# Two layers with three mixers on one core: the shared key and gate-rank product with both weight parts side by side, the latents' squares added on GpSimd, and another order of steps

## The chip, the cores and the metric

The kernel runs on one core of a Trainium2 chip. Its time is the device time of one execution in microseconds. The trace is one execution taken by the hardware profiler; its span is the time from the first to the last instruction that it records.

## What is computed

Two layers (256 tokens, width 1024, fp32). Each layer normalises x, multiplies it with one wide matrix, feeds the pieces to three mixers (latent attention, a gated linear attention, a state space mixer), adds the three under gates, and ends with a feed-forward part. Cut to what the change touches:

```python
h = rms_norm(x, norm1_g[l])
z = h @ w_in[l]
(cq, ckv, kpe, gq, gk, gv, glr, gr, su, gates) = split_in(z)   # 384, 256, 32, 256, 256, 512, 16, 512, 512, 3072
...
q = (rms_norm(h_cq, q_norm_g) @ w_uq).reshape(B, L, MLA_HEADS, MLA_QK)
kv = (rms_norm(h_ckv, kv_norm_g) @ w_ukv).reshape(B, L, MLA_HEADS, MLA_NOPE + MLA_V)
k = jnp.concatenate([k_nope, jnp.broadcast_to(k_pe[:, :, None, :], ...)], axis=-1)
...
log_a = jax.nn.log_sigmoid(g_lr.astype(f32) @ w_gate.astype(f32) + b_gate.astype(f32)) / GLA_TAU
```

kpe is the part of the keys that all heads of the latent attention share, glr the 16 numbers per token from which the gates of the linear attention come, cq and ckv the latents whose mean squares the two inner normalisations need.

## The kernel before

**Products in parts.** An fp32 number is kept as two fp32r parts, hi and lo. A product of two such numbers is three matmuls: hi by hi, hi by lo and lo by hi (`mm3`, L184 to L186, called by `ws` for one 128-column piece of weights). The activations h lie transposed, 128 rows by 256 tokens, in 8 pieces, both parts beside each other in `h2`; the normalisation's factor per token is multiplied in after the product (`rb`, the factors spread over 128 rows). In ff1 one 512-column matmul takes both parts of h at once (`wide`, L206), and a 256-column one adds the weights' lo part (L210).

**Weights.** They come as chunks of 128 rows by up to 1024 columns. `fetch` issues the transfer on SyncE's queue, `prep` makes hi with a cast on ScalarE (L164) and lo with a subtraction on VectorE (L165). Rings of 3 raw and 4 hi and lo buffers hold them; a chunk is prepared 3 chunks ahead of its use.

**Order.** Each mixer is cut into steps, and two strings of step names (`STEPS`, L1171, one per layer) say in which order the steps are given to a list scheduler; a number behind a name (`kg~53`) moves the step's instructions in the scheduler's priorities by so much. A step is one call of a generator up to its next `yield`. `P` is a step of the state space mixer's preparation (`s5_pre`), which computes the powers of its matrix and spreads them over block matrices with copies on ScalarE (`bbar`, `cmat`, L418) that TensorE then transposes (`Btp`, L453). In layer 1 it has run ahead of the steps shown.

**What the change touches.** `gla_qk` (step qk) makes the linear attention's queries and keys and `rb` (`norm_rows`). `kpe_glr` (step kg) computes kpe and glr in one product `kgp` of 128 weight columns, of which 48 are used (L682 on): 24 matmuls of 256 columns, one VectorE product by `rb` into `kgT` (L687), two transposes of its first 32 rows (kpe, L690). `gla_gate` (step gate) multiplies rows 32 to 47 of `kgT` with the gate weights (gatep, L937), and goes on to the exponentials ep, en, ab and the decay factors (L945 to L964), which need a table load on ScalarE where the function changes (L947, L948, L956). `att_c` (steps ckv, cq) computes a latent in 2 or 3 pieces of 128 columns (cp), squares each on ScalarE (sqc, L706), splits it into parts, and sums the squares over the 128 rows and the pieces with products by a column of ones into `stp` (L712): nk products for each of the two token tiles. R (L606) is the state space mixer's copy on GpSimd. Behind it ukv's products follow (kp, vp), and uq's (qp).

Of the kernel before, what the change touches and what calls it, by code (L numbers as in the profile page):

```python
# [19 lines left out]
D = 1024  # L20
# [36 lines left out]
CCOLS = {"uq": 768}  # L57
# [29 lines left out]
class Kern:  # L87
# [67 lines left out]
    def prep(self, k):  # L155
# [5 lines left out]
        hi = self.ring.tile([128, CW], F32R, tag="hi", name="hi", bufs=self.NHI)  # L161
        lo = self.ring.tile([128, CW], F32R, tag="lo", name="lo", bufs=self.NHI)
# [101 lines left out]
    def setup(self):  # L264
# [20 lines left out]
        nc.gpsimd.memset(self.ones, 1.0)  # L285
        self.half = c.tile([128, 1], F32, name="half")
# [395 lines left out]
    def kpe_glr(self, l):  # L682
        nc = self.nc
        p = self.pt("kgp", [128, L], tag="g")
        self.ws(p, self.w(l, ("kg", 0)), 0, self.h, KD)
        self.kgT = self.rp("kgT")
        nc.vector.tensor_tensor(out=self.kgT[0:48], in0=p[0:48], in1=self.rb[0:48], op=ALU.mult)  # L687
        p = self.pt("kpe", [128, NT, 32])
        for t in range(NT):
            nc.tensor.transpose(p[:, t, :], self.kgT[0:32, t * 128:(t + 1) * 128], self.ident[0:32, 0:32])  # L690
        self.kpe = self.tiny.tile([128, NT, 32], F32, tag="kpe", name="kpe", bufs=1)
        nc.scalar.copy(self.kpe, p)

    def att_c(self, l, nm):
# [13 lines left out]
        self.cT[nm] = [[c[:, m, 0], c[:, m, 1]] for m in range(nk)]  # L708
        pst = self.pt("stp", [128, NT])
        for t in range(NT):  # L710
            for m in range(nk):
                nc.tensor.matmul(pst[:, t:t + 1], lhsT=sq[m][:, t * 128:(t + 1) * 128], rhs=self.ones[:, 0:1],  # L712
                                 start=m == 0, stop=m == nk - 1)
# [189 lines left out]
    def gla_qk(self, l):  # L903
        nc = self.nc
        P = [self.pt("gqkp", [128, L], tag="g" if i < 2 else "acc") for i in range(4)]
        self.ws4(P, [self.w(l, ("gq", i)) for i in range(2)] + [self.w(l, ("gk", i)) for i in range(2)])
        self.norm_rows()
# [24 lines left out]
    def gla_gate(self, l):  # L932
# [3 lines left out]
        for m in range(2):  # L936
            nc.tensor.matmul(p[:, m, :], lhsT=wg[32:48, m * 128:(m + 1) * 128], rhs=self.kgT[32:48], start=True, stop=True)  # L937
# [211 lines left out]
    def ff2_end(self, l, n, po):  # L1149
# [232 lines left out]
```

## Time and profile before

| | us |
|---|---|
| median of 3 runs | 882.65 |
| lowest, highest | 882.17, 882.91 |
| the profiled execution | 882.19 |
| its span | 880.4 |
| TensorE busy | 861.7 |
| VectorE busy | 694.5 |
| ScalarE busy | 522.0 |
| GpSimd busy | 25.4 |

Busy times are of the span; engines work side by side. A row of a timeline gives start, duration, engine, line, operation and operands; matmuls overlap, so what one costs is the distance to the next start, not its duration. In brackets stands how long the engine was idle ahead of it and what ended that. PE is TensorE, PEld its weight loads, DVE VectorE, ACT ScalarE, POOL GpSimd.

### The profile page before, as it was taken

What the parts mean: (1) busy time and instruction counts of PE and PEld (TensorE: products, weight loads), DVE (VectorE), ACT (ScalarE), POOL (GpSimd) and SP (SyncE); (2) the same over time, 40 slices, a digit from 0 to 9 for tenths busy, and PEclk for the clock granted to TensorE, in tenths of its full rate; (3) what the DMA queues carried; (4) which work ended last, traced back from release to release, by engine and by line L of the source; (5) the groups of instructions that cost most, each with busy time, mean ns of one, the idle gap of its engine ahead of it and who ended that gap; (6) DMA issues with size and microseconds to landing.
All of it is one profiled execution on the core that took longest, in us unless ns stands there. A gap on an engine that the chain in (4) does not pass through costs nothing.

```text
span 880.4 us, 15290 instructions
## 1 busy us (share of the span) xinstructions
PE 861.7 (98%) x5900; PEld 771.2 (88%) x5900; DVE 694.5 (79%) x1339; ACT 522.0 (59%) x818; POOL 25.4 (3%) x35
## 2 busy tenths in 40 slices
PE   7999999999999999999999999999999999999998
PEld 6889988899988888888888989898999888888886
DVE  7999999987767986996677887899877776666664
ACT  6877887654456575664457647874554654444442
POOL 2000001010000000000000000002000000000000
PEclk9999999999999999999999999999999999999999
DMA  7534434245564565566545544244555555555562
GB/s 265 188 118 143 154 121 145 72 153 177 189 210 153 186 212 168 182 189 203 190 146 168 191 146 150 97 144 135 178 166 170 191 181 192 189 189 188 192 190 92
DMA packets 42264, 147.73 MB, mean 168 GB/s; under 512 B 4688, under 2 KB 5328, under 8 KB 42192
## 3 DMA queue, kind: packets, MB, share of 16 engines
q1 hardware_dynamic: 42192, 146.76, 51.6%
q8 instruction: 46, 0.75, 0.3%
q14 instruction: 26, 0.21, 0.1%
HBM read 145.70 MB, written 1.05 MB: 167 GB/s over the span
## 4 chain that ended last, share of the span: by engine, by line
PE 84%; DVE 10%; ACT 3%; issue 2%; DMA 1%; SPq 0%; DVEq 0%
PE fp L206 14%; PE fp L210 7%; PE fo L184 7%; PE fo L186 7%; PE fo L185 7%; PE gp L184 3%; DVE lo L165 3%; PE gp L185 3%; PE gp L186 3%; PE brp L184 2%; PE brp L186 2%; PE brp L185 2%; PE wo L186 2%; PE wo L184 2%; PE wo L185 2%
## 5 line engine op out<-in xcount | busy, mean ns | idle before, releaser
L165 DVE TENSOR_TENSOR lo<-raw,hi 128x1024 fp32r<-128x1024 f32 (+2 forms) x276 | 333.0, 1208 | 118.6 <-ACT hi L164 117.5
L164 ACT CAST hi<-raw 128x1024 fp32r<-128x1024 f32 (+2 forms) x276 | 286.1, 1038 | 234.0 <-PE fo L186 52.9
L206 PE MATMUL fp<-h,hi 128*128 128x512 f32 x512 | 180.5, 398 | 0.0
L210 PE MATMUL fp<-h,lo 128*128 128x256 f32 x512 | 133.5, 281 | 0.0
L184 PE MATMUL gp<-h,hi 128*128 128x256 f32 x384 | 109.9, 292 | 1.0 <-ACT ppt L875 0.8
L206 PEld LDWEIGHTS fp<-h,hi 128*128 128x128 f32 x512 | 93.9, 188 | 18.1
L186 PE MATMUL gp<-h,lo 128*128 128x256 f32 x384 | 107.8, 286 | 0.0
L185 PE MATMUL gp<-h,hi 128*128 128x256 f32 x384 | 107.4, 285 | 0.0
L210 PEld LDWEIGHTS fp<-h,lo 128*128 128x128 f32 x512 | 96.8, 189 | 5.5
L184 PE MATMUL fo<-hi,r 128*128 128x512 f32 x256 | 100.1, 391 | 0.0
L186 PE MATMUL fo<-hi,r 128*128 128x512 f32 x256 | 99.7, 390 | 0.0
L185 PE MATMUL fo<-lo,r 128*128 128x512 f32 x256 | 99.7, 389 | 0.0
L184 PEld LDWEIGHTS gp<-h,hi 128*128 128x128 f32 x384 | 72.7, 192 | 2.9 <-ACT ppt L875 1.0
L185 PEld LDWEIGHTS gp<-h,hi 128*128 128x128 f32 x384 | 72.6, 191 | 1.0 <-issue 0.5
L186 PEld LDWEIGHTS gp<-h,lo 128*128 128x128 f32 x384 | 72.7, 192 | 0.1
L185 PEld LDWEIGHTS fo<-lo,r 128*128 128x128 f32 x256 | 48.1, 188 | 10.1
L186 PEld LDWEIGHTS fo<-hi,r 128*128 128x128 f32 x256 | 48.1, 188 | 10.2
L184 PEld LDWEIGHTS fo<-hi,r 128*128 128x128 f32 x256 | 48.1, 188 | 8.8
L1133 ACT COPY fa<-fp 128x256 f32<-128x256 f32 x64 | 23.4, 367 | 29.3 <-PE fp L206 29.1
L1134 DVE TENSOR_TENSOR fa<-fa,fp 128x256 f32<-128x256 f32 x64 | 26.2, 416 | 13.7 <-ACT fa L1133 13.7
L1071 ACT ACTIVATE gt<-gt,hgateb 128x256 f32<-128x256 f32 x48 | 21.9, 501 | 9.0 <-DVE gt L1068 8.8
L256 ACT CAST r<-fa 128x512 fp32r<-128x512 f32 x32 | 19.9, 622 | 9.7 <-DVE fa L1135 9.5
(396 smaller groups left out, 1768.0 us busy)
## 6 DMA issues: line engine op xcount, KB each, us to landing
raw<-wst SPq DMA_DIRECT2D x266, 512.0 KB, 3.6
raw<-wst SPq DMA_DIRECT2D x6, 384.0 KB, 3.0
x<-xin SPq DMA_DIRECT2D x4, 256.0 KB, 4.6
raw<-wst SPq DMA_DIRECT2D x4, 256.0 KB, 5.6
bc_raw<-bcin SPq DMA_DIRECT2D x4, 256.0 KB, 3.8
out_dram<-x SPq DMA_DIRECT2D x4, 256.0 KB, 2.0
par<-parin SPq DMA_DIRECT2D x2, 205.0 KB, 5.8
masks<-consts SPq DMA_DIRECT2D x1, 128.0 KB, 3.8
```

Source lines behind the costliest of these rows:

```text
L164: nc.scalar.copy(hi[:, h], raw[:, h])
L165: nc.vector.tensor_tensor(out=lo[:, h], in0=raw[:, h], in1=hi[:, h].bitcast(F32), op=ALU.subtract)
L184: mm(out, lhsT=lt[0], rhs=rt[0], start=start, stop=False)
L185: mm(out, lhsT=lt[0], rhs=rt[1], start=False, stop=False)
L186: mm(out, lhsT=lt[1], rhs=rt[0], start=False, stop=stop)
L206: up = lambda: mm(flat, lhsT=w[0][:, c], rhs=self.h2[:, k].rearrange("p i t -> p (i t)"), start=k == 0, stop=k == KD - 1)
L210: mm(out[:, 0, :], lhsT=w[1][:, c], rhs=self.h[k][0], start=False, stop=False)
L256: nc.scalar.copy(hi, src)
L1071: nc.scalar.activation(g[:, m, :], g[:, m, :], AF.Tanh, scale=0.5, bias=self.small[l]["gateb"][:, c:c + 1])
L1133: nc.scalar.copy(a[:, m], p[:, 1, :])
L1134: self.mark = v.tensor_tensor(out=a[:, m], in0=a[:, m], in1=p[:, 0, :], op=ALU.add)
```

## The change

It has four parts.

The kg chunk holds 64 weight columns per piece instead of 128 (512 columns of the chunk in all, 256 KB). `prep` writes its hi and lo parts side by side, 64 columns each, into one tile, so that one 512-column matmul per piece multiplies both parts of the weights with both parts of h: 8 matmuls instead of 24. It also yields the product of the two lo parts, which was left out before. Adding up follows: ScalarE copies the half that belongs to h's lo part into `kgT`, VectorE adds the other half and multiplies by `rb`, all over 128 rows. The sum of hi and lo rows is left to the next products: kpe comes from two products with `fold` (ones where a row belongs to a column, in both halves; made in `setup` by one VectorE addition), and the gate weights stand in two places (rows 32 and 96), so that gatep sums over 128 rows.

The squares of a latent's pieces are added on GpSimd (one addition of 128x256 for ckv, two for cq), and one product per token tile sums over the rows.

`gla_qk` is cut in two steps: the products, and from `norm_rows` on.

Both strings of steps are new.

```diff
-CCOLS = {"uq": 768}
+CCOLS = {"uq": 768, "kg": 512}
...
+        if c[0] == "kg":
+
+            two = hi.rearrange("p (k i c) -> p k i c", i=2, c=64)
+            src = raw[:, 0:n].rearrange("p (k c) -> p k c", c=64)
+            nc.scalar.copy(two[:, :, 0], src)
+            nc.vector.tensor_tensor(out=two[:, :, 1], in0=src, in1=two[:, :, 0].bitcast(F32), op=ALU.subtract)
+            return hi, None
...
+        self.fold = c.tile([128, 32], F32, name="fold")
+        nc.vector.tensor_tensor(out=self.fold, in0=self.ident[:, 0:32], in1=self.ident[:, 64:96], op=ALU.add)
...
-        p = self.pt("kgp", [128, L], tag="g")
-        self.ws(p, self.w(l, ("kg", 0)), 0, self.h, KD)
+
+        p = self.pt("kgp", [128, 2, L], tag="g")
+        w, _ = self.w(l, ("kg", 0))
+        for k in range(KD):
+            nc.tensor.matmul(p.rearrange("p i t -> p (i t)"), lhsT=w[:, k * 128:(k + 1) * 128],
+                             rhs=self.h2[:, k].rearrange("p i t -> p (i t)"), start=k == 0, stop=k == KD - 1)
         self.kgT = self.rp("kgT")
-        nc.vector.tensor_tensor(out=self.kgT[0:48], in0=p[0:48], in1=self.rb[0:48], op=ALU.mult)
+        nc.scalar.copy(self.kgT, p[:, 1, :])
+        nc.vector.tensor_tensor(out=self.kgT, in0=self.kgT, in1=p[:, 0, :], op=ALU.add)
+        nc.vector.tensor_tensor(out=self.kgT, in0=self.kgT, in1=self.rb, op=ALU.mult)
+
         p = self.pt("kpe", [128, NT, 32])
         for t in range(NT):
-            nc.tensor.transpose(p[:, t, :], self.kgT[0:32, t * 128:(t + 1) * 128], self.ident[0:32, 0:32])
+            nc.tensor.matmul(p[:, t, :], lhsT=self.kgT[:, t * 128:(t + 1) * 128], rhs=self.fold, start=True, stop=True)
...
+        for m in range(1, nk):
+            nc.gpsimd.tensor_tensor(out=sq[0], in0=sq[0], in1=sq[m], op=ALU.add)
         pst = self.pt("stp", [128, NT])
         for t in range(NT):
-            for m in range(nk):
-                nc.tensor.matmul(pst[:, t:t + 1], lhsT=sq[m][:, t * 128:(t + 1) * 128], rhs=self.ones[:, 0:1],
-                                 start=m == 0, stop=m == nk - 1)
+            nc.tensor.matmul(pst[:, t:t + 1], lhsT=sq[0][:, t * 128:(t + 1) * 128], rhs=self.ones[:, 0:1],
+                             start=True, stop=True)
...
         self.ws4(P, [self.w(l, ("gq", i)) for i in range(2)] + [self.w(l, ("gk", i)) for i in range(2)])
+        yield
         self.norm_rows()
...
-            nc.tensor.matmul(p[:, m, :], lhsT=wg[32:48, m * 128:(m + 1) * 128], rhs=self.kgT[32:48], start=True, stop=True)
+            nc.tensor.matmul(p[:, m, :], lhsT=wg[:, m * 128:(m + 1) * 128], rhs=self.kgT, start=True, stop=True)
...
-        "qk P~-60 kg P~68 P~-15 gv~42 gate~30 P P~-2 P~15 gv su0 P P~-30 su0~-30 gv gv core~-8 ckv core~-98 P "
+        "qk qk~120 P kg P~68 P~-15 P gv~42 gate~30 P~-10 gv P su0 P P~-30 su0~-30 gv gv core~-16 ckv core~-98 "
```

In the rows of an order stand the line, the operation, out and inputs, and how often it follows itself. Line numbers of the changed kernel are a few higher (L186 becomes L193). The first pair is TensorE's order in layer 0 from the end of the product kgp on, before:

```order
L186 MATMUL kgp<-h,lo 128x256
L186 MATMUL gvp<-hi,h 128x512
L184 MATMUL gvp<-hi,h 128x512
L185 MATMUL gvp<-lo,h 128x512
L186 MATMUL gvp<-hi,h 128x512
L690 MATMUL kpe<-con,kgT 128x32 x2
L937 MATMUL gatep<-kgT,par 128x256 x2
```

And after:

```order
L193 MATMUL gvp<-hi,h 128x512
L697 MATMUL kgp<-h,hi 128x512 x8
L191 MATMUL gvp<-hi,h 128x512
L192 MATMUL gvp<-lo,h 128x512
L193 MATMUL gvp<-hi,h 128x512
L191 MATMUL gvp<-hi,h 128x512 x2
L192 MATMUL gvp<-lo,h 128x512 x2
L193 MATMUL gvp<-hi,h 128x512
L706 MATMUL kpe<-fold,kgT 128x32 x2
L955 MATMUL gatep<-kgT,par 128x256 x2
```

Between kgp and kpe stood four matmuls of gvp, and now stand eight. The second pair is TensorE's order in layer 0 from the last cp matmul of the step cq on, before:

```order
L186 MATMUL cp<-h,lo 128x256
L712 MATMUL stp<-ones,sqc 128x1 x2
L184 MATMUL vp<-hi,ckv 128x512
L185 MATMUL vp<-lo,ckv 128x512
L186 MATMUL vp<-hi,ckv 128x512
L184 MATMUL vp<-hi,ckv 128x512
L185 MATMUL vp<-lo,ckv 128x512
L712 MATMUL stp<-ones,sqc 128x1 x4
L186 MATMUL vp<-hi,ckv 128x512
```

And after:

```order
L193 MATMUL cp<-h,lo 128x256
L191 MATMUL vp<-hi,ckv 128x512
L192 MATMUL vp<-lo,ckv 128x512
L193 MATMUL vp<-hi,ckv 128x512
L191 MATMUL vp<-hi,ckv 128x512
L192 MATMUL vp<-lo,ckv 128x512
L193 MATMUL vp<-hi,ckv 128x512
L191 MATMUL vp<-hi,ckv 128x512
L729 MATMUL stp<-ones,sqc 128x1 x2
```

Of the six products of stp two are left, and seven matmuls of vp stand between the last cp and the first of them, where five stood ahead of the last four. The third pair is ScalarE's order in layer 0 around the spreads of bbar, which Btp needs, before (ep, en and dec are exponentials of the step gate; hi is the cast of a weight chunk):

```order
L948 ACTIVATE ab<-ab,half 128x512
L164 CAST hi<-raw 128x1024
L956 ACT_TABLE_LOAD
L956 ACTIVATE ep<-cs 128x512
L957 ACTIVATE en<-cs 128x512
L960 ACTIVATE dec<-cs 128x8
L164 CAST hi<-raw 128x1024
L418 ACTIVATE bbar<-z_476 64x16x16 x4
L164 CAST hi<-raw 128x1024
L418 ACTIVATE bbar<-z_477 64x16x16 x4
L418 ACTIVATE cmat<-z_478 64x16x16 x2
L958 ACTIVATE ab<-mn 128x512
```

And after:

```order
L966 ACTIVATE ab<-ab,half 128x512
L171 CAST hi<-raw 128x1024 x2
L427 ACTIVATE bbar<-z_463 64x16x16 x4
L171 CAST hi<-raw 128x1024
L427 ACTIVATE bbar<-z_464 64x16x16 x4
L427 ACTIVATE cmat<-z_465 64x16x16 x2
L974 ACT_TABLE_LOAD
L974 ACTIVATE ep<-cs 128x512
L427 ACTIVATE cmat<-z_465 64x16x16 x2
L975 ACTIVATE en<-cs 128x512
L976 ACTIVATE ab<-mn 128x512
L978 ACTIVATE dec<-cs 128x8
```

The table load with the three operations behind it moved from ahead of the first spread to behind the last one of bbar. On GpSimd a new instruction of the kind ISA stands directly behind the first copy of R and its memset in layer 0, ahead of the first addition.

## Rows read from the trace of the kernel before

**Rows 1.** The page, engines: busy us, share of the span, instructions.

```profile
PE 861.7 (98%) x5900; PEld 771.2 (88%) x5900; DVE 694.5 (79%) x1339; ACT 522.0 (59%) x818; POOL 25.4 (3%) x35
```

**Rows 2.** Stretches: us, busy of each engine (instructions), granted clock, DMA share, GB/s.

```profile
25.00:50.00 25.00, 22.84 (x136) 19.70 (x135) 23.35 (x79) 22.18 (x36) 0.72 (x2) 0.94 0.44 143
...
125.00:150.00 25.00, 23.08 (x184) 21.78 (x183) 24.98 (x53) 17.94 (x42) 3.37 (x3) 1.00 0.51 163
...
475.00:500.00 25.00, 25.00 (x188) 22.18 (x187) 19.09 (x44) 18.29 (x28) 0.00 (x0) 1.00 0.49 162
```

**Rows 3.** Timeline of TensorE, layer 0, end of kgp: start, duration, line.

```profile
28.44 0.28 PE L184 MATMUL kgp<-h,hi 128*128 128x256 f32 x1
28.56 0.28 PE L185 MATMUL kgp<-h,hi 128*128 128x256 f32 x1
...
29.27 0.39 PE L185 MATMUL gvp<-lo,h 128*128 128x512 f32 x1
29.50 0.40 PE L186 MATMUL gvp<-hi,h 128*128 128x512 f32 x1
```

**Rows 4.** Timelines of VectorE and TensorE around kgT and kpe, layer 0.

```profile
29.04 0.40 DVE L687 TENSOR_TENSOR kgT<-kgp,rb 48x256 f32<-48x256 f32 x1
...
29.83 0.25 PE L690 MATMUL kpe<-con,kgT 32*128 32x32 f32 x1
...
29.92 0.22 PE L690 MATMUL kpe<-con,kgT 32*128 32x32 f32 x1
```

**Rows 5.** The tile stp, and TensorE's weight loads in layer 0, step cq.

```profile
L712 PE MATMUL stp<-ones,sqc x40: 165/250/251, 71.6 to 526.3; 128*128 128x1 f32 x40
...
85.17 1.09 PEld L712 LDWEIGHTS stp<-ones,sqc 128*128 128x128 f32 x8
...
86.18 0.19 PEld L186 LDWEIGHTS vp<-hi,ckv 128*128 128x128 f32 x1
```

**Rows 6.** Timelines of GpSimd and VectorE: copies of R, and a neighbour.

```profile
33.40 0.61 POOL L606 COPY R<-s5r 128x512 f32<-128x512 f32 x1 [20.15 <-DVE s5r L349]
...
148.18 3.92 POOL L606 COPY R<-s5r 128x512 f32<-128x512 f32 x1 [20.85 <-DVE arec L877]
...
603.90 4.40 POOL L606 COPY R<-s5r 128x512 f32<-128x512 f32 x1 [18.13 <-DVE rot L620]
...
151.55 0.69 DVE L1068 TENSOR_TENSOR gt<-gp,rb 128x512 f32<-128x512 f32 x1
```

**Rows 7.** Timelines around the last squares: layer 0 cq, layer 1 ckv.

```profile
84.61 0.38 ACT L706 ACTIVATE sqc<-cp 128x256 f32<-128x256 f32 x1
...
84.77 0.95 DVE L165 TENSOR_TENSOR lo<-raw,hi 128x768 fp32r<-128x768 f32 x1
...
493.75 0.38 ACT L706 ACTIVATE sqc<-cp 128x256 f32<-128x256 f32 x1
493.87 1.23 DVE L165 TENSOR_TENSOR lo<-raw,hi 128x1024 fp32r<-128x1024 f32 x1 [0.70 <-ACT hi L164]
```

**Rows 8.** Timelines and stretch around Btp in layer 0.

```profile
38.42 1.28 ACT L956 ACT_TABLE_LOAD   x1
...
41.28 1.04 ACT L164 CAST hi<-raw 128x1024 fp32r<-128x1024 f32 x1
...
44.05 1.04 ACT L164 CAST hi<-raw 128x1024 fp32r<-128x1024 f32 x1
45.00 1.71 ACT L418 ACTIVATE bbar<-z 64x256 f32<-64x256 f32 x4
...
45.93 1.17 PE L453 MATMUL Btp<-con,bbar 128*128 128x128 f32 x8 [2.16 <-issue]
...
48.18 0.41 PE L184 MATMUL cp<-h,hi 128*128 128x256 f32 x1
48.39 0.42 PE L185 MATMUL cp<-h,hi 128*128 128x256 f32 x1
...
46.00:50.00 4.00, 4.00 (x20) 3.71 (x21) 3.54 (x7) 3.90 (x9) 0.00 (x0) 0.59 0.00 0
```

More of the change, by code (lines that the diff above doesn't have):

```diff
@@ L1191, in table @@
         T = {
-            "qk": ([r("gq", 2) + r("gk", 2)], self.gla_qk), "kg": (e("kg", 1), self.kpe_glr), "gate": ([[]], self.gla_gate),
+            "qk": ([r("gq", 2) + r("gk", 2), []], self.gla_qk), "kg": (e("kg", 1), self.kpe_glr), "gate": ([[]], self.gla_gate),
             "gv": (e("gv", 4), self.gla_vr, "gv"), "gr": (e("gr", 4), self.gla_vr, "gr"), "core": ([[]] * 3, self.gla_core),
@@ L1285, in pack_inputs @@
         ukv = [ukv[:, :, 0:64].reshape(256, 512), ukv[:, :, 64:128].reshape(256, 512)]
-        kg = np.concatenate([part("kpe", 32), part("glr", 16), np.zeros((D, 80), f)], axis=1)
+        kg = np.concatenate([part("kpe", 32), part("glr", 16), np.zeros((D, 16), f)], axis=1)
         for c, (n, i) in enumerate(CHUNKS):
@@ L1290, in pack_inputs @@
             elif n == "kg":
-                p = pack_ws(kg, 0)
+                p = pack_as(kg, 0, KD, 0, 64)
             elif n in ("gv", "gr"):
@@ L1327, in pack_inputs @@
         put(l, "gk96", a["mla_k_head_g"][l][:, None])
-        put(l, "wgate", a["gla_w_gate"][l], 32)
+        for o in (32, 96):
+            put(l, "wgate", a["gla_w_gate"][l], o)
         put(l, "gqr", np.broadcast_to(a["mla_q_head_g"][l][64:], (128, 32)))
```

24 rows, old and new, of the table STEPS are left out of this document.

## The prediction

> **What bounds the kernel now.** I read the engines' busy times first, then the table of stretches, then single rows. The reader is to see that TensorE is busy 861.7 of 880.4 us, so the kernel ends when TensorE's list is worked off; only 18.7 us of idle time are left in the span [rows 1]. Most of a change's worth is therefore TensorE time taken out of that list, minus the idle time that the change opens. The stretches tell where idle time is near: VectorE is full (24.98 of 25.00 us) in 125 to 150 us, where TensorE is busy for 23.08, and it has room at 475 to 500 us (19.09), where TensorE does not stop at all [rows 2]. The edits lie at 25 to 90 us and at 470 to 530 us, outside the stretch where VectorE is full, so what they add to VectorE or take from it has no price of its own; it counts where TensorE waits for one result.
>
> All sums are made against the profiled execution: 882.19 us, a span of 880.4 and 1.8 around it. The median of the three runs is 882.65, which is 0.46 above; I add that at the end.
>
> **kg product.** Before, each layer has 24 matmuls of 256 columns, which follow each other by 0.12 us (28.44, 28.56). Now there are 8 of 512 columns, and a 512-column matmul advances the list by 0.23 us (29.27, 29.50) [rows 3]. 48 x 0.12 = 5.8 us become 16 x 0.23 = 3.7: **-2.1**. Both figures come from the same place in the list, so I see no second answer. The halves of the old fetch, cast and subtraction go too (512 columns instead of 1024); they lie on queues that here run ahead of TensorE, and I cost them at nothing.
>
> **kpe.** The two transposes per layer advance by 0.09 us (29.83, 29.92) [rows 4]; now there are two fp32 products over 128 rows, and the nearest row for an fp32 product, stp, has two passes for each product of the program (40 records for the 20 that two layers hold), 8 passes taking 1.01 us (85.17 to 86.18), 0.126 each [rows 5]. 8 x 0.126 - 4 x 0.09 = **+0.6**. gatep keeps its count; its rows are 128 instead of 16, and stp shows that a pass of 128 rows has the same weight load. Nothing.
>
> **kgT.** Before: one VectorE product of 0.40 us stands between the last kgp matmul and kpe, and kpe waits 0.1 us for it in each layer: the last matmul ahead of it starts at 29.50 and advances by 0.23, kpe starts at 29.83 [rows 3, 4]; layer 1 has the same 0.1. After: a ScalarE copy, a VectorE addition and a VectorE product, each standing in a queue with other work. For 128x256 I take 0.38 us (the square, ScalarE) and 0.40 twice: 1.2 us in place of 0.4, plus what is queued. By the order of TensorE (first pair under the change), 8 gvp matmuls (1.8 us) cover it in layer 0. A cast of 1.0 us that the copy or a subtraction of 1.2 us that the addition falls behind breaks the cover. Placing the three by hand among their neighbours in the order I get waits of 0.7 us in layer 0 and 0.5 in layer 1, against 0.2 now: **+1.0**, between 0 and 2.5 (one cast and one subtraction in the way).
>
> **stp.** From 40 passes to 16: 24 x 0.126 = **-3.0**. What it is paid with is a GpSimd addition between the last square and stp. The trace of before has no such addition. The nearest row is GpSimd's copy of 128x512, 0.61 us when alone, but 3.92 us at 148.18: that one lasts over four VectorE products and a subtraction whose operands are both in SBUF, and ends when VectorE goes to a product that reads PSUM (151.55) [rows 6]. So the price of an addition is what VectorE does at that moment. [...]
> The cover is the TensorE work between the last cp matmul and stp. In the order after it is 15 cp (1.8 us) for ckv and 7 vp (1.6) for cq in layer 0 (for cq the second pair shows it), and by the same count 2.1 and 1.8 in layer 1. What must fit in: the square's wait for ScalarE, its 0.38 us, and the addition. Before, at the three places where I looked (two stand in the rows, layer 1's cq is like them), a weight subtraction runs at the time of the last square and ends behind it: at 85.72 against 84.99 for cq in layer 0, at 495.10 against 494.13 for ckv in layer 1 [rows 7]. It reads two SBUF operands, the kind that held the copy up. If the addition waits for its end and then takes 0.4 to 0.6 us, TensorE waits about 0.1, 0.9, 1.0 and 1.1 us. I take **+3.0** for the four; ends 0 (additions slip in ahead) and 5 (the next subtraction gets in front once).
> [...]
>
> **The reorder.** TensorE waits 2.16 us ahead of Btp at 45.93, whose last operand is a bbar spread on ScalarE (45.00, behind a cast at 44.05). [...] Of 4.0 us at 0.59, 0.41 x 4.0 = 1.6 us is time that the full clock would save: the gap is worth **3.8**. In the order before, a table load, ep, en and dec (38.42 to 41.28, 2.86 us) stand ahead of both sets of spreads; after, the load and ep stand behind both, en and dec further on (third pair). That frees the spreads by more than the 2.16 us, if z from VectorE keeps up. But ep, en and the Ap products, which need them, come later, and the subtraction for the next ckv chunk stands behind them on VectorE, so TensorE may wait there instead, with the same clock loss. Ends -3.8 and 0; I take **-2.0**. The other swaps in the two tables move steps whose inputs are long done (TensorE is idle for 0.00 us in 475 to 500 [rows 2]); cost nothing, bounds -1 to +1.
>
> Sum: -2.1 + 0.6 + 1.0 - 3.0 + 3.0 - 2.0 = **-2.5**: 879.7 for the profiled execution, **880.1** beside the median.
>
> **The rivals.**
> The cover holds everywhere: the additions slip in, no wait. -5.5: 877.2, and 875.4 if the Btp gap goes whole as well. For it: GpSimd has nothing else to do. Against it: the subtraction beside three of three squares. Taken as 876.5, chance 0.16.
> No change: TensorE's 4.5 us are saved, and the waits for the additions and for kgT give 4.0 back, while the Btp gap only moves to Ap (0): -0.5, 882.2. For it: VectorE is busy 23.35 of 25.00 us in 25 to 50 us [rows 2], and the moved products are on it. Chance 0.24.
> Slower: the additions behave as the copy at 148.18, held over several VectorE instructions. The place is stp of ckv and cq. At 3.9 instead of 0.6 us, 3.2 us each at two of the four and 1.0 at two: 8.4 in place of 3.0, so +2.9: 885.5. It turns the sign when the four waits add up to more than 5.5 us, 1.4 each. Against it: by the order after, behind that subtraction VectorE has an operation on PSUM, the split of cp, at which the addition can get in. Chance 0.11.
> [...] In the order GpSimd has a new instruction of the kind ISA right behind the first R copy and its memset, and the additions some rows on; if it is not done by then, layer 0's first stp waits. From the end of that copy (34.01 [rows 6]) to the first stp (71.6 now [rows 5]) it has over 35 us, so I give it 0.04. [...] At a wait as long as the longest R copy's, 4.4 us [rows 6], less the 0.1 counted there, the time would be 884.4.
>
> **How the numbers follow.** Forecast 0.45, with its own range 878.3 to 882.0 (kgT and reorder to either side). Something like 0.2% (1.8 us) can be told from no change, so faster means under 880.9. The forecast gives 0.32 of its 0.45 to faster, 0.13 to the same; the first rival all of its 0.16; the second 0.08 to faster (part of the gap goes after all), 0.14 to the same and 0.02 to slower; the last two go to slower with 0.13 of 0.15. Faster 0.56, same 0.29, slower 0.15. The range leaves out the lower half of the first rival (0.08) and most of the last two (0.12): 876.2 to 884.0.
>
> **What would show it.** kgp: 16 matmuls that advance by 0.23 us; anything near 0.46 fells the largest sure term. stp: 16 passes, and the idle time ahead of them, put down to GpSimd, is the +3.0: four gaps of about 0 to 1 us. The additions' own durations tell whether VectorE holds them: 0.4 to 0.6 alone, 1 and more beside a subtraction. kpe: idle time ahead of it of about 0.7 us in layer 0 and 0.5 in layer 1. Btp: the 2.16 us gone and the clock whole in 45 to 50 us, or a gap of its size at Ap or at the first cp. If TensorE's busy time falls by less than 4 us, the costs in the list are wrong; if by 4 to 6 with the time unchanged, the waits are.

## The result: slower by 0.7%, and the profile after

| us | before | after |
|---|---|---|
| median of 5 runs each | 882.65 | 889.14 |
| lowest, highest | 881.88, 883.22 | 886.54, 891.48 |
| profiled execution, its span | 882.19, 880.4 | 889.14, 887.1 |

The ratio is 1.0072 with the interval 1.0057 to 1.0087: 6.5 us slower, where 2.5 faster was forecast. The time lies outside the range, 5.1 us above its upper end, and on the other side. The five executions of the new kernel spread over 5 us and go with the clock that TensorE was granted: 886.54 at 0.998 of full speed, 891.48 at 0.990. So a part of the loss is the clock's, and that part changes from one execution to the next. Medians and ratios here leave out three slow runs (938.08 of before, 937.73 of e14, 2980.16 of e16).

The page's line of engines after the change, to be held against [rows 1]:

```profile
PE 861.7 (97%) x5848; PEld 769.4 (87%) x5848; DVE 696.4 (78%) x1342; ACT 519.9 (59%) x820; POOL 31.4 (4%) x41
```

TensorE is busy 861.7 us in both kernels, so nothing seems to have left its list. But busy time has two parts, the list and what a lower clock adds to it. The stretches of the new kernel (span, then busy time of PE, PEld, DVE, ACT, POOL, then the granted clock, DMA share, GB/s):

```profile
25.00:50.00 25.00, 19.96 (x116) 17.00 (x115) 22.77 (x78) 21.00 (x35) 0.72 (x2) 1.00 0.31 108
...
50.00:54.00 4.00, 3.43 (x13) 2.88 (x14) 3.99 (x5) 3.44 (x9) 0.00 (x0) 0.50 0.42 140
54.00:58.00 4.00, 4.00 (x30) 3.65 (x29) 1.42 (x3) 0.98 (x1) 0.00 (x0) 0.68 0.77 253
76.00:82.00 6.00, 6.00 (x37) 5.80 (x37) 4.26 (x18) 1.70 (x4) 0.00 (x0) 0.72 0.44 147
134.00:140.00 6.00, 5.92 (x35) 5.88 (x36) 5.26 (x16) 3.95 (x12) 0.00 (x0) 0.72 0.65 225
...
475.00:500.00 25.00, 24.24 (x162) 21.35 (x161) 18.47 (x26) 19.20 (x29) 1.11 (x1) 1.00 0.51 160
```

In three stretches the clock that TensorE was granted lay below 1 (0.50 to 0.72). In before, where it was 0.50 (48 to 50 us), cp matmuls of 256 columns advance by 0.21 us [rows 8]; those of kgp, at 1.00, by 0.12 [rows 3]. By my estimate the time lost in a stretch is its busy time times what the clock lacks of 1: 3.43 x 0.50 + 4.00 x 0.32 = 3.0, and 1.7 in each of the other two, 6.4 in all, against 1.6 in the one such stretch before [rows 8]. Idle time grew from 18.7 to 25.4. So +6.7 idle and +4.7 from the clock stand against -4.7 of the list, and the span is 6.7 longer. The list's share is only what is left over, and it is good to no better than some 3 us: worked out alike for three kernels with the same instructions (after, e5, e9) it comes to 855.3, 857.6 and 858.5 us, since the ends of matmuls at a gap are modelled. The idle time and the clock are what I go by.

Where the new idle time lies, from the view of waits of TensorE after (line waited for, then us in total, times, longest):

```profile
PE stp L729 <- POOL sqc L726: 4.0, 4, 1.3
...
PE cp L193 <- DVE lo L172: 3.5, 1, 3.5
PE s L882 <- DVE amx L887: 2.0, 1, 2.0
...
PE gp L191 <- DVE gt L1086: 1.8, 2, 1.0
PE kgp L697 <- DVE gqk L928: 1.5, 1, 1.5
...
PE Btp L462 <- issue: 0.6, 1, 0.6
```

These waits fill the stretches: in 25 to 50 us TensorE is busy for 19.96 of 25.00 (22.84 in [rows 2]); the missing 5.0 are the waits at kgp (1.5), at Btp (0.6) and the part of the one at cp that lies before 50 us (2.9). In 475 to 500 us, where TensorE did not stop before, 0.76 are the start of a wait at stp.

In layer 0 the slow stretch at 50 us follows the wait of 3.5 at cp, the one at 76 us the first wait at stp, the one at 134 us the wait of 2.0 at s. The wait at kgp is there with the old product too, in other executions: 0.74 in e8, 1.16 in e4. I count it to neither side. The wait at s goes with the new strings: it is in all seven profiles that have them together with the new kg form (2.0 to 2.9 us in after, e2, e5, e6, e7, e9, e10), and in none with the old ones. Other waits of before went in exchange: from 100 to 445 us TensorE is idle for 3.5 us in after and 4.6 in before, so with the 1.7 of clock this stretch costs +0.6, inside the -1 to +1 that the prediction gave to the other swaps.

### The profile page after: what moved, and what is told of

Read it like the earlier page. It is cut to its first block, busy times and chain, and to the rows that moved or that the text cites. A ratio compares the mean times of both kernels' runs of the same rounds, so it can differ in the third digit from the quotient of the medians.

```text
span 887.1 us, 15202 instructions
## 1 busy us (share of the span) xinstructions
PE 861.7 (97%) x5848; PEld 769.4 (87%) x5848; DVE 696.4 (78%) x1342; ACT 519.9 (59%) x820; POOL 31.4 (4%) x41
## 4 chain that ended last, share of the span: by engine, by line
PE 77%; DVE 11%; ACT 7%; DMA 2%; issue 2%; POOL 1%; SPq 0%; ACTq 0%; DVEq 0%; POOLq 0%
PE fp L213 14%; PE fp L217 7%; PE fo L191 7%; PE fo L193 7%; PE fo L192 7%; DVE lo L172 4%; PE gp L191 3%; PE gp L193 3%; PE gp L192 3%; PE brp L191 2%; PE brp L193 2%; PE brp L192 2%; DMA raw<-wst 2%; ACT hi L171 2%; PE wo L191 2%
## 5 line engine op out<-in xcount | busy, mean ns | idle before, releaser
L193 PE MATMUL gp<-h,lo 128*128 128x256 f32 x384 | 107.8, 287 | 0.0
L193 PE MATMUL fo<-hi,r 128*128 128x512 f32 x256 | 99.6, 389 | 0.0
L193 PEld LDWEIGHTS gp<-h,lo 128*128 128x128 f32 x384 | 73.1, 193 | 0.5 <-issue 0.4
L193 PEld LDWEIGHTS fo<-hi,r 128*128 128x128 f32 x256 | 48.0, 188 | 10.2
L1151 ACT COPY fa<-fp 128x256 f32<-128x256 f32 x64 | 23.4, 367 | 28.5 <-PE fp L213 28.3
L193 PE MATMUL cp<-h,lo 128*128 128x256 f32 x80 | 23.8, 298 | 3.5 <-DVE lo L172 3.5
```

The costliest lines, as they stand in the source:

```text
L193: mm(out, lhsT=lt[1], rhs=rt[0], start=False, stop=stop)
L1151: nc.scalar.copy(a[:, m], p[:, 1, :])
```

## The experiments

The kernel before ran again beside each group: 882.8 to 882.9. "Idle" is the span less TensorE's busy time, "clock" the time lost to a granted clock below 1, worked out as above from stretches of 2 us; both are of the one profiled execution, the medians of all.

| kernel | median | ratio, 95% | idle | clock |
|---|---|---|---|---|
| before | 882.65 | | 18.7 | 1.7 |
| e8, before again | 882.29 | (one run) | 20.0 | 0.0 |
| after | 889.14 | 1.0057 to 1.0087 | 25.4 | 6.4 |
| e1, after in the old order | 899.73 | 1.0172 to 1.0199 | 31.7 | 9.4 |
| e2, after without additions | 886.04 | 1.0022 to 1.0047 | 22.0 | 4.9 |
| e3, kg form alone | 891.49 | 1.0083 to 1.0112 | 26.5 | 3.3 |
| e4, additions alone | 886.20 | 1.0029 to 1.0055 | 25.0 | 0.0 |
| e5, after, gate later | 891.17 | 1.0085 to 1.0123 | 29.2 | 1.7 |
| e6, e5 and stp later | 891.26 | 1.0082 to 1.0108 | 28.5 | 3.3 |
| e7, additions on VectorE | 887.87 | 1.0046 to 1.0070 | 24.6 | 1.5 |
| e9, after, gate sooner | 890.87 | 1.0064 to 1.0101 | 24.8 | 3.3 |
| e10, e9 without additions | 887.72 | 1.0039 to 1.0063 | 22.0 | 3.1 |
| e11, before, more on VectorE | 888.01 | 1.0046 to 1.0072 | 22.8 | 1.7 |
| e12, before, more on TensorE | 889.25 | 1.0059 to 1.0083 | 19.4 | 0.0 |
| e13, before, stp in one pass | 881.54 | 0.9977 to 0.9994 | 19.6 | 0.0 |
| e14, before, kg form in layer 1 | 884.70 | 1.0012 to 1.0037 | 21.7 | 0.0 |
| e15, before, gate later | 884.24 | 1.0007 to 1.0024 | 21.7 | 0.0 |
| e16, before's steps in the new order | 885.28 | 1.0007 to 1.0028 | | |

### One part at a time: e1 to e4

e2 is the changed kernel with the squares summed by TensorE as before:

```diff
-        for m in range(1, nk):
-            nc.gpsimd.tensor_tensor(out=sq[0], in0=sq[0], in1=sq[m], op=ALU.add)
...
-            nc.tensor.matmul(pst[:, t:t + 1], lhsT=sq[0][:, t * 128:(t + 1) * 128], rhs=self.ones[:, 0:1],
-                             start=True, stop=True)
+            for m in range(nk):
+                nc.tensor.matmul(pst[:, t:t + 1], lhsT=sq[m][:, t * 128:(t + 1) * 128], rhs=self.ones[:, 0:1],
+                                 start=m == 0, stop=m == nk - 1)
```

> The changed kernel without the additions: stp again takes 40 passes over all squares. Theory A: stp's 24 more passes cost 3.0 us, the four waits (4.0) and the slow stretch at 76 to 82 us (1.7) go: 889.1 - 2.7 = 886.4, and the wait for the subtraction at 50.6 us stays at 3.5. Theory B, the additions are the whole loss: 882.6 or less.

e4 puts the additions alone into the kernel before (the same lines, in the other direction):

> The kernel before with the additions on GpSimd alone, old order and old kg. By the waits seen in the changed kernel (4.0 us in four gaps, additions of 1.4 to 1.7 us beside a subtraction) less 3.0 us of passes: 883.7, and 885.4 if a slow stretch of 1.7 us follows a gap again. Rival, the additions only wait so long because of the new order's neighbours: the four gaps sum to under 1.5 us, 881 or less.

Without the additions the new kernel gains 3.1 us, as forecast for e2; with them the old one loses 3.3, which is above both forecasts for e4, and no slow stretch is there to explain it. Both signs are clear, and e9 less e10 gives 3.15 for a third order of the work; each figure is known to some 1.5 us. So in the changed kernel the additions cost 3 us where I forecast +3.0 - 3.0 = 0. It is not a price that they carry everywhere: e1 less e3, below, are the additions in the new code with the old strings, and there they cost 8.2, with 7.1 us of waits at stp (1.9 in e3) and 6.1 us more of clock. A small part lies outside the span: an execution takes 2.0 us more than its span in after, e1, e4, e5 and e6, 2.3 in e9, and 1.8 in every kernel without additions on GpSimd. What fills it is not shown. In e2 the wait at cp and the clock behind it stay (0.50 in 50 to 54 us), while the clock in 76 to 82 us is whole (1.00). This wait and stretch of e2:

```profile
50.51 0.58 PE L193 MATMUL cp<-h,lo 128*128 128x256 f32 x1 [3.48 <-DVE lo L172]
...
76.00:82.00 6.00, 6.00 (x39) 5.47 (x39) 5.99 (x27) 3.49 (x7) 0.00 (x0) 1.00 0.37 98
```

e1 is the changed kernel with the two order strings of before (its first step written "qk qk", since it is now cut in two), e3 the same with the kg form alone, without the additions:

```diff
-        "qk qk~120 P kg P~68 P~-15 P gv~42 gate~30 P~-10 gv P su0 P P~-30 su0~-30 gv gv core~-16 ckv core~-98 "
+        "qk qk P~-60 kg P~68 P~-15 gv~42 gate~30 P P~-2 P~15 gv su0 P P~-30 su0~-30 gv gv core~-8 ckv core~-98 P "
...
```

> All of the new code with the strings of steps of the kernel before (qk's two steps one behind the other). Theory A, the new order costs most: its three places (TensorE waits 3.5 us for a subtraction at 50.6 and runs slow behind it, 1.5 us for kgp at 26.6, a slow stretch behind the wait at 134) go, and the Btp gap of before (3.8 with its slow stretch) returns: 889.1 - 6.5 = 882.6, between 881.5 and 884. Theory B, the additions on GpSimd cost most: 887 to 889, the four waits ahead of stp stand at some 4 us and the rest does not change.

> The old order and stp as before, only the kg product in its new form (kgp, kgT, kpe, gatep). Theory A: TensorE's list is 1.5 us shorter, no new wait at kpe: 881.1 (880.5 to 882). Rival: the wait of 1.5 us ahead of kgp belongs to the new kg form itself, not to the order: 882.6 or above, with the wait there again.

e1 lies far above both its forecasts. e3 loses 8.6 us where 1.5 of gain was expected. It falls under the rival's open "882.6 or above", and the wait at kgp is there (1.2), but that is a small part of 8.6. Its profiled span is 9.2 longer than that of before, 6.3 of it by the end of layer 0. There a wait that [rows 8] does not have stands at the second half of Btp, on the tile that ScalarE copies after the first half:

```profile
51.03 0.66 PE L462 MATMUL Btp<-con,bbar 128*128 128x128 f32 x4 [3.39 <-ACT Bt L463]
```

So the new order is worth 10.6 us to the changed code (e1 less after) and 5.5 to the kg form alone (e3 less e2), and the kg form with its order still loses 3.1 (e2 less the 882.9 that ran beside it). That the order alone is worth -2.0, to be added to the other terms, was the wrong way to ask: an order suits one set of durations.

### The additions' place, and the wait at cp: e5, e6, e7, e9, e10

e5 and e9 are the changed kernel with one number in the first string, which moves the gate's instructions in the scheduler's priorities; e6 adds a move of stp to e5, e10 takes the additions out of e9:

```diff
-        "qk qk~120 P kg P~68 P~-15 P gv~42 gate~30 P~-10 gv P su0 P P~-30 su0~-30 gv gv core~-16 ckv core~-98 "
+        "qk qk~120 P kg P~68 P~-15 P gv~42 gate~45 P~-10 gv P su0 P P~-30 su0~-30 gv gv core~-16 ckv core~-98 "
```

(e9: `gate~0`.) In e6:

```diff
-        for t in range(NT):
-            nc.tensor.matmul(pst[:, t:t + 1], lhsT=sq[0][:, t * 128:(t + 1) * 128], rhs=self.ones[:, 0:1],
-                             start=True, stop=True)
+        with self.later(60):
+            for t in range(NT):
+                nc.tensor.matmul(pst[:, t:t + 1], lhsT=sq[0][:, t * 128:(t + 1) * 128], rhs=self.ones[:, 0:1],
+                                 start=True, stop=True)
```

e7 does the additions on VectorE instead of GpSimd:

```diff
-            nc.gpsimd.tensor_tensor(out=sq[0], in0=sq[0], in1=sq[m], op=ALU.add)
+            nc.vector.tensor_tensor(out=sq[0], in0=sq[0], in1=sq[m], op=ALU.add)
```

> The changed kernel with one number of layer 0's string altered (gate~30 to gate~45): on VectorE the subtraction for the ckv chunk then stands ahead of the product that makes ep, and on ScalarE a copy of Bt ahead of the table load. Theory A, the wait of 3.5 us for that subtraction and the slow stretch of 3.0 us behind it are the main loss: both go, 889.1 - 6.5 = 882.6 (881.5 to 884). Rival, the wait only moves, to the second Btp or to Ap, as in the run with the kg part alone (3.4 us): 888 to 889, with a gap of 3 us or more between 45 and 60 us.

> The same, and the stp products moved back by 60 in priority: by the order 1.1, 1.15, 0.9 and 2.0 us more of TensorE work stand ahead of them. If the additions cost only their wait, the four gaps (4.0 us) shrink to under 0.5 and the slow stretch of 1.7 us at 76 us goes: 877.5 (876.5 to 879.5), faster than the kernel before. Rival, what needs stp (the factors of k, v and q) is then late instead: 881 to 883, with new gaps behind the moved products.

> The changed kernel with the six additions on VectorE (0.42 us each) instead of GpSimd; the rest of the order stays nearly the same. [...] Rival, the addition waits behind the same subtraction in VectorE's own queue: gaps within 0.5 us of those with GpSimd, 888 to 889.

> The changed kernel with one number of layer 0's string altered the other way (gate~30 to gate~0): cs, ep, en and their table load stand ahead of the spreads of bbar again, as in the kernel before, and 24 matmuls of cp and 12 of grp ahead of Btp. Theory C, the new kg form makes the gate's chain late (cs at 44.7 instead of 38.9 us), and the waits at 45 to 53 us with the slow stretch follow from that: no wait over 1 us there, 889.1 - 5 = 884 (883 to 886). Rival, from 25 to 210 us VectorE's list sets the pace and waits only change places, as in the two runs with the gate later: 888 to 891, the time ahead of layer 1 unchanged.

> The same without the additions on GpSimd (stp again over all squares). Theory C with the additions' price of 3.1 us as measured: 881 (880 to 882.5), faster than the kernel before by the kg form's 1.5 us. Rival, VectorE's pace: within 1 us of 886.0, what the changed kernel took without the additions.

In e5 the wait at cp is gone, and the kernel is 2 us slower than after. Its waits:

```profile
PE stp L729 <- POOL sqc L726: 5.4, 4, 2.2
...
PE s L882 <- DVE amx L887: 2.3, 1, 2.3
PE Ap L995 <- DVE en L981: 2.0, 1, 2.0
```

What was one wait is now several, on other operands. e9 gets rid of it the other way and waits 2.4 at Btp and 2.9 at s. e6 shortens stp's waits (one of 1.14 is left), and glup waits 2.18 and s 2.27. e7 has no wait at stp at all, so the rival, that an addition waits as long behind the subtraction in VectorE's own queue, is out. It gains 1.3 of the 4.0 that the four waits were (by the medians, the intervals overlap), and its wait at cp is still 3.5. e10, with the gate sooner and no additions, is no faster than e2. So the theory "one gap, taken away, gives its size back" falls in each of the five: with the gap gone the order against the queues of VectorE and ScalarE is another, and other results come late. Nor is e9 less e10 all waiting: where both ran at a granted clock of 0.996 they differ by 0.9 to 1.1 us (888.87 against 887.73 and 887.98).

### What sets the pace there: e11 and e12

If VectorE's queue set the pace of that stretch, more work on it would cost its length, and more work on TensorE nothing. e11 adds 15 VectorE products in layer 0 of the kernel before, three behind each cp product, e12 60 matmuls:

```diff
+            if l == 0:
+                junk = self.sm.tile([128, 512], BF16, tag="junk", name="junk", bufs=1)[:, 0:L]
+                for _ in range(3):
+                    v.tensor_scalar(out=junk, in0=p, scalar1=2.0, scalar2=None, op0=ALU.mult)
```

```diff
-            self.ws(p, self.w(l, (nm, m)), 0, self.h, KD)
+            w = self.w(l, (nm, m))
+            if l == 0:
+                for k in range(4):
+                    self.mm3(p, [x[:, k * 128:(k + 1) * 128] for x in w], self.h[k], k == 0, k == 3)
+            self.ws(p, w, 0, self.h, KD)
```

> The kernel before with 15 more VectorE operations of 128x256 from PSUM in layer 0 (three for each piece of ckv and cq, their results unused), about 6.0 us of VectorE time between 50 and 90 us. If VectorE's list sets the pace there: 882.7 + 5 to 6 = 888 to 889. If TensorE's list does and VectorE has room: under 884.

> The kernel before with 60 more matmuls of 256 columns in layer 0 (the first half of each cp product is done twice, the first time for nothing), 7.2 us of TensorE time at the same place. If TensorE's list sets the pace: 882.7 + 7 = 889 to 890. If VectorE's list does, the waits up to 210 us take part of it up: 886 or less.

VectorE is busy for 5.0 us more in e11 than in before (699.5 against 694.5), which cost 5.1; TensorE for 7.4 more in e12 than in e8 (867.9 against 860.5, no clock lost in either), which cost 6.4. Work added to either list there is paid nearly in full, against the prediction's claim that what the edits add to VectorE there "has no price of its own". Which way it is paid is not shown: both runs have another order too, and in the program the added VectorE products stand ahead of the split of cp, on which later products wait.

### One part with the order nearly held: e8, e13 to e16

Of these, e13 and e14 hold the order nearly, and e15 and e16 change the order alone. e13 takes the passes away without an addition: the squares and the ones are fp32r, with which stp takes 20 passes instead of 40, and all else stays. e14 uses the kg form in layer 1 only (`kpe_glr1` is the changed `kpe_glr`). e15 is the kernel before with `gate~30` made `gate~45`; e16 is the kernel before with the new strings (and qk cut). e8 is the kernel before, profiled once more. The diffs of e13, e14 and e15; e16's strings are those of the change.

```diff
+        self.oner = c.tile([128, 2], F32R, name="oner")
+        nc.scalar.copy(self.oner, self.ones[:, 0:2])
...
-            sq.append(self.rp("sqc"))
+            sq.append(self.sm.tile([128, L], F32R, tag="rp", name="sqc", bufs=3))
...
-                nc.tensor.matmul(pst[:, t:t + 1], lhsT=sq[m][:, t * 128:(t + 1) * 128], rhs=self.ones[:, 0:1],
+                nc.tensor.matmul(pst[:, t], lhsT=sq[m][:, t * 128:(t + 1) * 128], rhs=self.oner,
```

```diff
-        n = CCOLS.get(c[0], CW)
+        n = 512 if (l, c[0]) == (1, "kg") else CCOLS.get(c[0], CW)
...
+        if l == 1:
+            return self.kpe_glr1(l)
```

```diff
-        "qk P~-60 kg P~68 P~-15 gv~42 gate~30 P P~-2 P~15 gv su0 P P~-30 su0~-30 gv gv core~-8 ckv core~-98 P "
+        "qk P~-60 kg P~68 P~-15 gv~42 gate~45 P P~-2 P~15 gv su0 P P~-30 su0~-30 gv gv core~-8 ckv core~-98 P "
```

> The kernel before, once more with a profile. In the changed kernel TensorE waits 1.5 us at 26.6 us for the product kgp (1.2, 1.0 and 1.2 in the experiments, also in the one with the old kg part), and ScalarE's cast ahead of it waits for a transfer. If the transfer's arrival in an execution makes this wait, the kernel before has it too: 1.0 to 1.5 us at 26 us, total 883 to 884. If the change makes it, none, as in the first profile.

> The kernel before with the squares of the latents kept as fp32r, so that each product of stp takes one pass instead of two; no additions, strings as before. By the order lists under 60 rows of an engine move. If TensorE's list is worth its length where the order stays: 20 passes of 0.126 us less, 882.7 - 2.5 = 880.2 (879.8 to 881). If time taken out of the list at these places is lost in waits anyway: 882 to 883.

> The kernel before with the new kg form in layer 1 only; the order of all engines stays but for the rows of kg itself (40 rows on TensorE, 8 on VectorE, 11 on ScalarE). If the form as such is what I priced: 24 x 0.12 - 8 x 0.23 = 1.0 us less, kpe's passes 0.3 more, a wait of 0 to 1.1 us for kgT: 882.0 to 883.1. If the form itself costs what the run with kg alone lost in both layers (8.6, 2.3 of it in layer 1): 885.

> The kernel before with one number of layer 0's string altered (gate~30 to gate~45), no operation changed; 35 to 70 rows of an engine move. If the order alone is worth several us, which is my theory for the loss beside the additions: 885 to 889, with new waits between 45 and 210 us. If not: 882 to 884.

> The kernel before with the changed kernel's strings and its cut of qk in two steps, all operations as before. If the new order is worse by itself: 886 or more, with the wait of 2 us or more for s near 131 us that all runs in the new order had. If it only fails to fit the new operations: 881 to 884.

e13 is the fastest kernel of the study: 881.54, ratio 0.9985 with the interval 0.9977 to 0.9994, 1.3 us below before where 2.5 was expected. The rows give a possible account of the missing part. TensorE of before, two and eight passes of stp with what follows:

```profile
71.62 0.28 PE L712 MATMUL stp<-ones,sqc 128*128 128x1 f32 x2
71.77 0.49 PE L184 MATMUL grp<-hi,h 128*128 128x512 f32 x1
...
525.56 0.95 PE L712 MATMUL stp<-ones,sqc 128*128 128x1 f32 x8
526.37 0.42 PE L184 MATMUL qp<-hi,cq 128*128 128x384 f32 x1
```

and of e13, four passes in place of the eight, and kpe:

```profile
470.87 0.24 PE L692 MATMUL kpe<-con,kgT 32*128 32x32 f32 x1 [0.85 <-DVE kgT L689]
...
524.64 0.58 PE L714 MATMUL stp<-oner,sqc 128*128 128x2 f32 x4
525.09 0.42 PE L184 MATMUL qp<-hi,cq 128*128 128x384 f32 x1
```

Eight passes advance the list by 0.81 us, two by 0.15: 0.10 and 0.07 a pass, not 0.126. Added up over all groups, stp takes 3.7 us in before, 1.7 in e13, 1.7 in after. So 2.0 were to be had, and a new wait of 0.85 at kpe (0.1 before) takes 0.7 of it: 1.3. Other waits differ as well between the two executions (kgp's 0.7 of e8 is not in e13), so this account fits and is not shown.

In e14 VectorE's and TensorE's orders of layer 1 stay nearly as they were, so that the rows can be set side by side. VectorE of before and then of e14, and TensorE of e14:

```profile
478.64 1.23 DVE L951 TENSOR_TENSOR_SCAN cs<-cmask,mn 128x512 f32<-128x512 f32 x1
```

```profile
481.33 1.23 DVE L982 TENSOR_TENSOR_SCAN cs<-cmask,mn 128x512 f32<-128x512 f32 x1
...
485.63 1.16 PE L1008 MATMUL Ap<-ep,en 64*128 64x128 f32 x16 [0.61 <-DVE en L994]
...
495.67 0.83 PE L742 MATMUL stp<-ones,sqc 128*128 128x1 f32 x6 [1.16 <-ACT sqc L736]
```

There is no wait at kpe. The gate's scan cs comes 2.7 us later, though kgp starts at the same time (467.43, and 467.49 in before): kgT is ready later, and gatep, the activations and the scan hang on it. TensorE pays at Ap (0.61), at stp (1.16) and at kgp (0.27), 2.04 in all, against some 0.75 less in its list: +1.3. The profiled execution is 1.3 longer than that of e8 (883.61 and 882.29, no clock lost in either), but layer 1 by itself is 1.8 longer, as the medians are (884.70 less 882.86); some 0.5 of it is in none of these three waits.

e15 shows what one number of the order does by itself: the gap ahead of Btp is 1.80 and the second half of Btp waits 1.88, +1.4 in all. e16's runs fall into two groups, 882.7 to 883.4 at a granted clock of 0.999 to 1.0 and 885.2 to 886.5 at 0.996 to 0.998. So the new order does nothing or 2.5 us to the old code, from one execution to the next. In e16's one trace TensorE is busy for 2969 us, so its times can't be set beside the others, but the order of its rows can; it is used below.

## Why the prediction was wrong

Two steps failed. The additions were put at nothing, their waits against the passes they save, and cost 3.1. The reorder was put at -2.0 with 0 as its worst end, and at its place it came to +3.3, because the result that TensorE needs next after the old gap comes later than before. The single terms in turn:

**kg product: right.** Eight matmuls take 1.95 us, 0.244 each (0.23 forecast). **kpe: right.** Its four passes take 0.44 us. TensorE of after, layer 0:

```profile
26.59 2.11 PE L697 MATMUL kgp<-h,hi 128*128 128x512 f32 x8 [1.55 <-DVE gqk L928]
28.54 0.39 PE L191 MATMUL gvp<-hi,h 128*128 128x512 f32 x1
...
30.36 0.60 PE L706 MATMUL kpe<-fold,kgT 128*128 128x32 f32 x4
30.80 1.11 PE L955 MATMUL gatep<-kgT,par 128*128 128x256 f32 x4
```

**kgT: wrong in its place.** I had a wait of 0.7 at kpe; there is none in layer 0, as the gvp matmuls cover it. But kgT has a second consumer, gatep, and behind it the longest chain of the stretch (activations with table loads, scan, ep, en), which I did not follow. It is the step that e14 prices in layer 1: 2.7 us later, +2.04 of waits at operations I had not named. The +1.0 was sized at the wrong consumer. In layer 1, where I had 0.5 at kpe, after has no wait there either, but e2 has 1.1 and e10 0.7.

**stp, the passes: mis-sized.** -3.0 became -2.0. I took 0.126 from the weight loads of the longest group [rows 5], where the distance to the next matmul was to be had from TensorE's own rows (0.80 for the same eight, 85.41 to 86.21).

**stp, the waits: right in kind, 4.0 instead of 3.0.** GpSimd, VectorE and TensorE of after at three of the four places:

```profile
73.58 1.22 DVE L172 TENSOR_TENSOR lo<-raw,hi 128x1024 fp32r<-128x1024 f32 x1
73.64 1.74 POOL L726 TENSOR_TENSOR sqc<-sqc 128x256 f32<-128x256 f32 x1 [38.83 <-ACT sqc L722]
75.44 0.60 PE L729 MATMUL stp<-ones,sqc 128*128 128x1 f32 x4 [1.33 <-POOL sqc L726]
...
91.15 0.73 POOL L726 TENSOR_TENSOR sqc<-sqc 128x256 f32<-128x256 f32 x1 [6.26 <-ACT sqc L722]
91.34 1.36 DVE L172 TENSOR_TENSOR lo<-raw,hi 128x768 fp32r<-128x768 f32 x1
91.94 0.61 PE L729 MATMUL stp<-ones,sqc 128*128 128x1 f32 x4 [0.35 <-POOL sqc L726]
...
500.42 0.38 PE L729 MATMUL stp<-ones,sqc 128*128 128x1 f32 x2 [1.15 <-POOL sqc L726]
```

The addition at 73.64 starts beside a subtraction, which ends at 74.80, and ends 0.58 behind it; the one at 91.15 came first, takes 0.73, and the subtraction takes 1.36 instead of the 0.95 of [rows 7]. The five additions of after that start behind the start of a subtraction last 1.42 to 1.74 and end 0.58 to 0.60 behind it. So in these rows what comes second lasts longer, and it ends 0.58 (the addition) and 0.82 (the subtraction) behind the first, less than the 0.73 and 0.95 that they take otherwise. That an addition takes 0.4 to 0.6 us once the subtraction has ended was my estimate, with no row of an addition to show it; the 0.58 to 0.60 are what the trace has in its place.

So the four stretches of stp give +4.0 - 2.0 = +2.0 (the small waits of before at these places left out), and the pairs of kernels 3.1 to 3.3. In after and e2 the rest is the clock (6.4 against 4.9); in e4 no clock is lost and the waits at stp are 2.9, so that some 2.4 of its 3.3 lie in idle time elsewhere that I can't put down to one place.

**The reorder: wrong in its bound.** I gave it -3.8 to 0 (the wait of 2.16 us and the 1.6 for the granted clock of 0.59 in 46 to 50 us [rows 8]), as if the gap at Btp could at worst move whole. Btp's gap did shrink from 2.16 to 0.59. The granted clock in 46 to 50 us is 0.97, but TensorE is busy there for only 1.10 of 4.00 us, so that is no gain. But VectorE, ScalarE and TensorE of after show what came instead; of before only two rows, the same scan and the product mn ahead of it:

```profile
37.50 0.69 DVE L949 TENSOR_TENSOR mn<-mn,ab 128x512 f32<-128x512 f32 x1 [0.64 <-ACT ab L948]
...
38.86 1.22 DVE L951 TENSOR_TENSOR_SCAN cs<-cmask,mn 128x512 f32<-128x512 f32 x1
```

```profile
39.06 0.69 DVE L967 TENSOR_TENSOR mn<-mn,ab 128x512 f32<-128x512 f32 x1 [0.33 <-ACT ab L966]
...
43.20 1.05 ACT L171 CAST hi<-raw 128x1024 fp32r<-128x1024 f32 x1
44.72 1.21 DVE L969 TENSOR_TENSOR_SCAN cs<-cmask,mn 128x512 f32<-128x512 f32 x1
...
46.73 1.28 ACT L974 ACT_TABLE_LOAD   x1
48.03 0.63 ACT L974 ACTIVATE ep<-cs 128x512 f32<-128x512 f32 x1
48.69 0.69 DVE L980 SCALAR_TENSOR_TENSOR ep<-gqk,ep 128x512 f32<-128x512 f32 x1 [1.84 <-ACT ep L974]
49.30 1.22 DVE L172 TENSOR_TENSOR lo<-raw,hi 128x1024 fp32r<-128x1024 f32 x1
50.57 0.58 PE L193 MATMUL cp<-h,lo 128*128 128x256 f32 x1 [3.47 <-DVE lo L172]
```

The cast of the chunk that cp reads is done at 44.25. Its subtraction waits until 49.30, because it stands on VectorE behind the product ep, which waits 1.84 for ScalarE, where the table load and ep now stand behind the spreads, and for cs, which is 5.9 us later than before. The prediction named this path ("the subtraction for the next ckv chunk stands behind them on VectorE, so TensorE may wait there instead") and then capped it at the old gap. Measured at this place: 0.6 + 3.5 + 3.0 of clock against 2.2 + 1.6, **+3.3** where -2.0 stood. This order of the rows, which I put down to the new strings, comes with the new kg form. Two runs show it: e3 has the old strings and the new form, e16 the new strings and the old form. VectorE and ScalarE of e3, then of e16:

```profile
44.01 1.71 ACT L427 ACTIVATE bbar<-z 64x256 f32<-64x256 f32 x4
44.58 1.22 DVE L968 TENSOR_TENSOR_SCAN cs<-cmask,mn 128x512 f32<-128x512 f32 x1
46.59 1.28 ACT L973 ACT_TABLE_LOAD   x1
```

```profile
90.64 1.22 DVE L952 TENSOR_TENSOR_SCAN cs<-cmask,mn 128x512 f32<-128x512 f32 x1
106.65 1.28 ACT L957 ACT_TABLE_LOAD   x1
109.00 1.68 ACT L418 ACTIVATE bbar<-z 64x256 f32<-64x256 f32 x4
```

With the new form the scan and the load stand late under both sets of strings; with the old form the load stands ahead of the spreads under both. One number of the string moves it either way: e9 has both early with the new form, and e15 has both late with the old one, which by itself costs 1.4. That the list scheduler makes this order out of the form's other durations is likely and not shown. Nor is most of the delay kgT's own: at the product mn ahead of the scan the chain is 1.6 us late (39.06 against 37.50), and the other 4.3 are products z that now stand ahead of the scan on VectorE. As times the two can't be added: alone, the strings cost 0 to 2.5 (e16) and the kg form 8.6 (e3), together 3.1 (e2).

**The sum.** Forecast -2.5; measured +6.5 = 3.1 (additions, after less e2) + 3.4 (kg form and order, e2 less before's 882.65). In the first, 0 stood for 3.1; in the second, -2.1 + 0.6 + 1.0 - 2.0 = -2.5 stood for 3.4.

**The rivals.** "Slower", by additions held over several VectorE instructions, had the right sign and the wrong mechanism: its four waits were to add up to more than 5.5, and they are 4.0 (in e1, with the old strings, they are 7.1). The last rival, with the new ISA instruction, did not show: what ended GpSimd's idle time ahead of the first addition is ScalarE's square, the addition's 1.74 are told by the subtraction beside it, and in e4 the first addition takes 0.75. "No change" had the right mechanism, a gap that moves on, but named Ap and had it no larger than before; that VectorE is nearly full in 25 to 50 us is not shown to be the reason, since it waits 1.84 us for ScalarE just ahead of the late subtraction.

## What to carry to other kernels

A changed operand is to be priced at every consumer, and the one with the longest chain behind it first; here that was gatep, not kpe. Where a hand-tuned order feeds a scheduler, changed operations can move rows far from the edit even with the same strings (e3), so the bound for "moved steps" must reach well above nothing, and a gap that closes is worth its size only if the next result in each queue is already there. A saving that nearly leaves the order and the queues alone (e13) is small, and most of it is kept.

## What the runs showed of the hardware

Behind a gap of the same size the clock fell in one execution and not in another. e8, the kernel before, in the row of Btp and the stretch behind it:

```profile
46.31 1.06 PE L453 MATMUL Btp<-con,bbar 128*128 128x128 f32 x8 [2.17 <-issue]
...
46.00:50.00 4.00, 3.06 (x23) 2.75 (x23) 3.53 (x8) 3.88 (x10) 0.00 (x0) 1.00 0.00 0
```

The same gap of 2.16 was followed by 0.59 in [rows 8]. So the 3.8 that I put on that gap was 2.2 in one execution and 3.8 in the other, though the two executions differ by 0.1 us in all. e4, e12 and e14 have the gap of 2.2 without a loss, e11 with one of 1.7. Behind the gaps of 3.4 to 3.5 us in after, e1, e2 and e3 the granted clock was 0.50 each time (50 to 54 us of after and e2, 54 to 58 of e1, 52 to 58 of e3); e7 has such a gap too, with 0.50 in 52 to 54 us and 0.80 in 54 to 56, and lost only 1.5 us there. What decides it is left open.

Nor is the price of a GpSimd operation beside VectorE a fixed one. The copy of R that took 3.92 us at 148.18 in [rows 6] takes 0.98 in e8, the same kernel:

```profile
147.85 0.98 POOL L606 COPY R<-s5r 128x512 f32<-128x512 f32 x1 [20.84 <-DVE arec L877]
```
